# The third unit of a SwiGLU's first phase as a two-sided unit: three of its eight pairs by seven products instead of eight

## The chip, the core and the metric

The kernel runs on one core of a Trainium2 chip, in one launch. The metric is the device time of that launch in microseconds; it took 2192.04 us as the median of three runs (2191.01 to 2192.64).

The engines meant below: TensorE (PE) multiplies a 128x128 stationary operand with up to 512 columns and adds into a bank of PSUM; VectorE (DVE) and ScalarE (ACT) work element by element and read the banks; SyncE (SP) issues the transfers (DMA) from the chip's memory, in order. There are eight banks of 128x512 f32. An engine takes its instructions in the order that was laid down when the program was built, and waits at an instruction until what it needs is there.

## The reference, cut to what matters

Two layers on 256 tokens of width 2048. Each has a mixer and then a SwiGLU of hidden width 5632, in float32. The change is inside the SwiGLU:

```python
def swiglu(x, w_gate, w_up, w_down):
    return (jax.nn.silu(x @ w_gate) * (x @ w_up)) @ w_down

x = layer_norm(DN_ALPHA * x + y, ln_mix_g[layer], ln_mix_b[layer])
f = swiglu(x, ffn_w_gate[layer], ffn_w_up[layer], ffn_w_down[layer])
x = layer_norm(DN_ALPHA * x + f, ln_ffn_g[layer], ln_ffn_b[layer])
```

## The kernel before, in words

Float32 precision is kept by splitting: a weight piece `raw` is copied by ScalarE into a rounded `whi` (L127), VectorE makes the rest `wlo = raw - whi` (L128), and x is held in the same two parts (xTh, xTl). A product is then three matmuls, lo x hi, hi x hi and hi x lo (`mm3`, L292). The 256 tokens are two groups of 128 ("tok").

The hidden width is cut into eleven **units** of 512 columns, and these into three phases (`PHASES`): units 0 to 2, 3 to 6, 7 to 10. A phase computes its units (gate and up projection, silu, product, transposed into yT) and then its share of the down projection, n = 0 to 3, which is added to the residual.

A unit needs 16 k tiles of 128 rows for gate and for up. It goes by eight **pairs** of k tiles. The first phase's units are "whole" (`whole`): eight **halves** (weight pieces of 128x1024, 0.5 MB: two k tiles of one side) for gate, then eight for up, twelve matmuls to a half. The units of the other phases are "two-sided" (`unit`, L454 on): gate and up of a pair are handled together, into four sums c11, c21, c12, c22 (token by side). Three of the pairs (`SEVEN` = 5, 6, 7; two in a phase's last unit) are done by seven products in place of eight, a 2x2 scheme over (two tokens) x (two sides). They need forms of x (sums and differences of x's quarters, `forms_of`, made once a layer and kept) and of the weights (`load_seven`), and four more sums p1, p5, p6, p7:

```python
raw = sp.tile([P, 4, NCH], F32, tag="rs", name="rs", bufs=1)
z = sp.tile([P, 4, NCH], F32, tag="z", name="z", bufs=1)
last_load[0] = nc.sync.dma_start(raw, src).ins
nc.scalar.copy(hi[:, :3], raw[:, :3])
nc.vector.tensor_tensor(z[:, :2], raw[:, 0:3:2], raw[:, 3:4].to_broadcast([P, 2, NCH]), op=add)
nc.vector.tensor_tensor(z[:, 2], z[:, 0], raw[:, 2], op=add)
nc.vector.tensor_tensor(z[:, 3], z[:, 2], raw[:, 1], op=add)
nc.vector.tensor_tensor(lo[:, :3], raw[:, :3], hi[:, :3].bitcast(F32), op=sub)
split(hi[:, 3:], lo[:, 3:], z)
```

So a two-sided load is one transfer of 1 MB into `rs`, of which there is one buffer; three sums of 1024, 512 and 512 columns (L445 to L447); two copies on ScalarE (1536 and 2048 columns) and two splits on VectorE (1536 and 2048). The next load can go out when the last sum has read `rs`. Its parts `sh`, `sl` have two buffers. The forms of x lie in the tiles `xs` and `fs`, which share the buffers of `rs` and `z`, and are split into `fmh`, `fml`.

**Memory.** The weight halves use a ring of buffers: four in `wp`, and until the first phase's units are over seven more (layer 0; in layer 1 three more, and four that were kept) in a pool beside the mixer's room `mix_pool`, which also holds `gam`, `bet` and the tile `sil`. After the third unit `close_mix` gives that memory back, the pool `sp` for the two-sided units opens in it, and the forms of x are made in steps (`make`), spread over the halves of the first down phase. `raw` has four buffers.

**Banks.** PSUM is used in two ways (`open_banks`). In "uses": three `acc`, two `tr` (transposes), three `mx`. In "sides": four `aside` and four `bside`; a unit takes the four of one side for its c sums, and the other four serve first the transposes of the unit before and then p1, p6, p5, p7. The switch to "sides" comes after the third unit.

**Order.** A scheduler lays down each engine's queue when the program is built, by the order of the code and by priority: a load and its split stand some 400 instructions ahead of their place, as far as buffers allow, and `tc.high_priority(offset=1000)` moves other parts forward. `issue_after(low[-1])` puts a piece behind the last split. `later` holds work that is due after so many halves (`half_done`): the transposes of a unit (`transpose4`), and `make`.

Of the kernel before, what the change touches and what calls it, by code (L numbers as in the profile page):

```python
# [11 lines left out]
F32 = mybir.dt.float32  # L12
# [6 lines left out]
P = 128  # L19
# [4 lines left out]
NCH = 512  # L24
# [42 lines left out]
HELD = 6  # L67
FREE = 7
PHASES = ((0, 1, 2), (3, 4, 5, 6), (7, 8, 9, 10))


SEVEN = (5, 6, 7)
PAIRS_FIRST = (0, 1, 2, 3, 5, 4, 6, 7)
PAIRS = (0, 1, 5, 2, 3, 6, 4, 7)
PAIRS_LAST = (0, 1, 5, 2, 6, 3, 4, 7)
# [5 lines left out]
def trunk(ctx: ExitStack, tc: tile.TileContext, a, out):  # L81
# [9 lines left out]
    def open_banks(kind):  # L91

        if banks:
            banks["stack"].close()
        stack = ctx.enter_context(ExitStack())
        pool = stack.enter_context(tc.tile_pool(name="ps", bufs=1, space=PSUM, reuse_waits="tile"))
        banks.update(stack=stack, pool=pool, kind=kind, side=0)
# [22 lines left out]
    def mxp():  # L120
        return bank("mx", 3)
# [26 lines left out]
    first = [True]  # L148
# [33 lines left out]
    later = []  # L182
# [91 lines left out]
    def transpose4(src, hi, lo, ahead_by=0):  # L274
        t = trp()
        for k in range(4):
            transpose(t[:, k * P : (k + 1) * P], src[:, k * P : (k + 1) * P], ident)
        v = t.rearrange("p (k t) -> p k t", k=4)
        with tc.high_priority(offset=ahead_by):
            split(hi, lo, v)  # L280
# [174 lines left out]
    def unit(sp, pairs, sevens, w, lhs, forms, yT, opening):  # L455

        b = {n: side_bank() for n in ("c11", "c21", "c12", "c22")}
        begun = set()
        left = {n: 4 * (len(pairs) - len(sevens)) // 2 for n in b}
        for _, _, n in SEVEN_ORDER:  # L460
            left[n] = left.get(n, 0) + len(sevens)

        def product(name, x, wt):
            left[name] -= 1
            mm3(b[name], x, wt, name not in begun, left[name] == 0)
            begun.add(name)

        behind = [low[-n] if opening and n else None for n in BEHIND]
        for p in pairs:
            if p in sevens:  # L470
                if "p1" not in b:
                    b.update((n, side_bank(True)) for n in ("p1", "p6", "p5", "p7"))
                wt = load_seven(sp, w[p], behind.pop(0))
                for i, x, name in SEVEN_ORDER:
                    product(name, forms[p][x], wt(i))
            else:
                for n, ks in ((0, (2 * p, 2 * p + 1)), (1, (2 * p + 1, 2 * p))):
                    hi, lo = load_half(w[p][:, 2 * n : 2 * n + 2])
                    for tok in range(NT):
                        for kk in range(2):  # L480
                            product(f"c{tok + 1}{n + 1}", lhs(tok, ks[kk]), (hi[:, kk, :], lo[:, kk, :]))
                    half_done()
        with tc.high_priority(offset=1000):
            g0, w_, v, x = (sp.tile([P, NCH], F32, tag=n, name=n, bufs=1) for n in ("g0", "g1", "u0", "u1"))
            nc.scalar.copy(g0, b["p1"])  # L485
            nc.vector.tensor_tensor(w_, g0, b["p6"], op=sub)
            nc.vector.tensor_tensor(v, w_, b["p5"], op=add)
            nc.vector.tensor_tensor(w_, w_, b["p7"], op=add)
            nc.vector.tensor_tensor(x, w_, b["p5"], op=add)
            nc.vector.tensor_tensor(g0, g0, b["c11"], op=add)  # L490
            nc.scalar.activation(g0, g0, AF.Silu)
            nc.vector.tensor_tensor(v, b["c12"], v, op=sub)
            nc.vector.tensor_tensor(w_, w_, b["c21"], op=add)
            nc.scalar.activation(w_, w_, AF.Silu)
            nc.vector.tensor_tensor(x, b["c22"], x, op=sub)

            banks["side"] ^= 1
            for tok, (g, u) in enumerate(((g0, v), (w_, x))):
                nc.vector.tensor_tensor(g, g, u, op=mult)
                s = slice(tok * P, (tok + 1) * P)  # L500
                later.append([2 + tok, lambda g=g, s=s: transpose4(g, yT[0][:, :, s], yT[1][:, :, s], 1000)])

    def ffn(layer, xT, res, mix_pool, close_mix, keep, last):
        lhs = x_lhs(xT)
        w = a[f"gu{layer}"]

        def whole(c, pool, first):

            gouts = [acc() for _ in range(NT)]
            sil = {}  # L510

            def silu(tok):
                sil[tok] = pool.tile([P, NCH], F32, tag="sil", name="sil", bufs=3)
                nc.scalar.activation(sil[tok], gouts[tok], AF.Silu)

            mm_chunk([(w[c, i][:, :2], (2 * i, 2 * i + 1)) for i in range(8)], lhs, gouts, tok_major=first, after=silu)

            uouts = [mxp() for _ in range(NT)]
            y = new_yT()

            def gated(tok):
                with tc.high_priority(offset=1000):
                    nc.vector.tensor_tensor(sil[tok], sil[tok], uouts[tok], op=mult)
                s = slice(tok * P, (tok + 1) * P)
                later.append([(2 if c == PHASES[0][-1] else 4) + tok, lambda: transpose4(sil[tok], y[0][:, :, s], y[1][:, :, s])])

            mm_chunk([(w[c, i][:, 2:], (2 * i + 1, 2 * i)) for i in range(8)], lhs, uouts, after=gated)
            return y

        stack = ExitStack()  # L530
        forms, making = {}, []

        def make():
            with tc.issue_after(low[-1]):
                if next(making[0], "end") is None:
                    later.append([3, make])

        nxt = cdp = None
        groups = {}
        for pi, chunks in enumerate(PHASES):  # L540
            end = pi == len(PHASES) - 1
            for c in chunks:
                if pi == 0:
                    groups[c] = whole(c, mix_pool, c == 0)
                else:
                    groups[c] = new_yT()
                    pairs = PAIRS_FIRST if c == chunks[0] else PAIRS_LAST if c == chunks[-1] else PAIRS
                    sevens = SEVEN[:-1] if c == chunks[-1] else SEVEN
                    unit(sp, pairs, sevens, w[c], lhs, forms, groups[c], c == chunks[0])
            if pi == 0:  # L550
                close_mix()
                sp = later_pool(stack, f"sp{layer}")
                open_banks("sides")
                making.append(forms_of(sp, xT, forms))
                later.append([2, make])
            gl = [groups[c] for c in chunks]
            if end:
                stack.close()
                open_banks("uses")
                cdp = None if last else keep("cdc")  # L560
                open_ring(keep(f"er{layer}"), 4)
                open_ring(later_pool(stack, f"e{layer}"), 3)
                fp = later_pool(stack, f"g{layer}")
                nxt = None if last else new_xT()
            stats = new_stats()
            evac, norm = residual_tools(res, None, None, None, stats)
            for n in range(4):
                if cdp and n == 1:
                    consts.extend(cd_constants(cdp))
                if end and n == 1:  # L570
                    evac, norm = residual_tools(res, *load_gb(fp, layer, "ffn"), stats)
                outs = [acc() for _ in range(NT)]
                halves = [(a[f"down{layer}"][n, 2 * c + i], two(4 * ci + 2 * i)) for ci, c in enumerate(chunks) for i in range(2)]

                def after(tok):
                    with tc.high_priority(offset=1000 if end and n == 3 else 0):
                        evac(tok, n, outs[tok], pi == 0, end)
                        if end and n == 3:
                            norm(tok, nxt, out if last else None)

                mm_chunk(halves, y_lhs(gl), outs, tok_major=(end and n == 3), after=after)
            if not end:
                banks["side"] ^= 1
        if end:
            rings.pop()
            stack.close()
        return nxt
# [416 lines left out]
    xT = new_xT()  # L1004
# [11 lines left out]
    def later_pool(stack, name):  # L1016
        return stack.enter_context(tc.tile_pool(name=name, bufs=1, reuse_waits="tile"))
# [22 lines left out]
    xT = layer_end(0, a["ab_out"], AB_OUT_GROUPS, yT, False)  # L1040
# [119 lines left out]
```

## Time and profile before

| | |
|---|---|
| median of three runs | 2192.04 us |
| the profiled execution's own time | 2190.72 us |
| its span on the core | 2188.9 us |
| granted TensorE clock, mean | 0.998 |
| PE busy | 2170.7 us (99%) |
| DVE busy | 1558.8 us (71%) |
| ACT busy | 1051.3 us (48%) |

The profile comes from one execution; its span starts with the program's first instruction on the core and ends with the last, and the time around it is 1.8 us more. Matmul records overlap, since a matmul's record holds its latency: what a matmul costs is read from one start to the next. In a row, `acc<-whi,xTl` says that a matmul reads whi and xTl and adds into acc; numbers of buffers are left out in the profile.

### The profile page before, as it was taken

The page shows a single profiled execution, that of the slowest core. Times are in us where ns is not written, and L with a number is a line of the kernel's source. Part 1 is how long each engine was busy: PE and PEld are TensorE (multiplying, and loading weights), DVE is VectorE, ACT ScalarE, POOL GpSimd, SP SyncE. Part 2 cuts the span into 40 slices and gives each one's busy share as a digit, 9 for nine tenths or more (in the row PEclk, how much of TensorE's full clock was granted, in tenths as well). Part 3 has the DMA queues.
Part 4 walks back from the last instruction along what each step waited for, and adds up shares of the span by engine and source line. Part 5 has one row for each costly group of instructions (what it writes and reads, how often), then busy time and mean ns, then how long its engine had stood idle before and what let it go on. Part 6 is the DMA issues. An engine that isn't in the chain of part 4 may idle for free.

```text
span 2188.9 us, 26626 instructions
## 1 busy us (share of the span) xinstructions
PE 2170.7 (99%) x10048; PEld 1804.7 (82%) x10048; DVE 1558.8 (71%) x1954; ACT 1051.3 (48%) x1278; POOL 51.7 (2%) x51
## 2 busy tenths in 40 slices
PE   9999999999999999999999999999999999999997
PEld 7888888888888888888888888888888888888886
DVE  6886688577537787577876776667367896768765
ACT  6445544545435455444545554455344554445442
POOL 0000000000000000000000300000000000000000
PEclk9999999999999999999999999999999999999999
DMA  8555546584736565565549553747456555655563
GB/s 294 161 164 180 167 132 190 195 287 138 237 125 219 188 208 189 189 230 185 199 157 305 165 190 106 235 150 253 143 187 232 185 187 188 222 173 200 172 238 122
DMA packets 112850, 420.64 MB, mean 192 GB/s; under 512 B 13776, under 2 KB 16848, under 8 KB 105808
## 3 DMA queue, kind: packets, MB, share of 16 engines
q1 hardware_dynamic: 112720, 418.93, 57.8%
q8 instruction: 79, 1.29, 0.2%
q14 instruction: 51, 0.42, 0.1%
HBM read 416.78 MB, written 2.10 MB: 191 GB/s over the span
## 4 chain that ended last, share of the span: by engine, by line
PE 96%; DMA 1%; DVE 1%; ACT 0%; issue 0%; SPq 0%; DVEq 0%; ACTq 0%
PE acc L292 41%; PE bside L292 23%; PE aside L292 21%; PE mx L292 7%; PE mx L729 1%; PE tr L124 1%; DMA raw<-in_down 1%; DVE wlo L128 0%; DMA rs<-in_gu 0%; PE mx L775 0%; DMA raw<-in_ab_in 0%; PE bside L124 0%; PE aside L124 0%; PE mx L985 0%; ACT whi L127 0%
## 5 line engine op out<-in xcount | busy, mean ns | idle before, releaser
L128 DVE TENSOR_TENSOR wlo<-raw,whi 128x1024 fp32r<-128x1024 f32 (+1 forms) x673 | 817.8, 1224 | 438.2 <-ACT whi L127 431.2
L127 ACT CAST whi<-raw 128x1024 fp32r<-128x1024 f32 (+1 forms) x673 | 703.7, 1052 | 820.5 <-PE acc L292 262.3
L292 PE MATMUL acc<-whi,xTl 128*128 128x512 f32 x864 | 342.8, 397 | 4.8 <-ACT whi L127 4.8
L292 PE MATMUL acc<-whi,xTh 128*128 128x512 f32 x864 | 340.0, 393 | 0.0
L292 PE MATMUL acc<-wlo,xTh 128*128 128x512 f32 x864 | 337.9, 393 | 0.1
L292 PE MATMUL acc<-whi,yTl 128*128 128x512 f32 x512 | 200.8, 392 | 0.2
L292 PE MATMUL acc<-whi,yTh 128*128 128x512 f32 x512 | 199.6, 390 | 0.0
L292 PE MATMUL acc<-wlo,yTh 128*128 128x512 f32 x512 | 197.7, 390 | 0.0
L292 PEld LDWEIGHTS acc<-whi,xTl 128*128 128x128 f32 x864 | 162.9, 189 | 37.2 <-ACT whi L127 5.7
L292 PEld LDWEIGHTS acc<-wlo,xTh 128*128 128x128 f32 x864 | 162.9, 189 | 33.9 <-DVE wlo L128 1.1
L292 PEld LDWEIGHTS acc<-whi,xTh 128*128 128x128 f32 x864 | 163.1, 189 | 31.1
L292 PE MATMUL bside<-whi,xTl 128*128 128x512 f32 x336 | 131.4, 391 | 0.7 <-ACT g L485 0.6
L292 PE MATMUL bside<-whi,xTh 128*128 128x512 f32 x336 | 131.0, 390 | 0.0
L292 PE MATMUL aside<-whi,xTl 128*128 128x512 f32 x336 | 131.0, 390 | 0.0
L292 PE MATMUL aside<-whi,xTh 128*128 128x512 f32 x336 | 130.9, 390 | 0.0
L292 PE MATMUL bside<-wlo,xTh 128*128 128x512 f32 x336 | 128.1, 390 | 0.0
L292 PE MATMUL aside<-wlo,xTh 128*128 128x512 f32 x336 | 128.1, 390 | 0.0
L292 PEld LDWEIGHTS acc<-wlo,yTh 128*128 128x128 f32 x512 | 96.1, 188 | 20.6 <-DVE wlo L128 0.5
L292 PEld LDWEIGHTS acc<-whi,yTl 128*128 128x128 f32 x512 | 96.2, 188 | 20.0 <-DVE res L310 0.5
L292 PEld LDWEIGHTS acc<-whi,yTh 128*128 128x128 f32 x512 | 96.2, 188 | 19.4
L128 DVE TENSOR_TENSOR sl<-z,sh 128x2048 fp32r<-128x2048 f32 x44 | 100.7, 2289 | 6.4 <-ACT sh L127 5.7
L292 PE MATMUL bside<-whi,yTl 128*128 128x512 f32 x256 | 99.8, 390 | 0.0
(266 smaller groups left out, 3414.3 us busy)
## 6 DMA issues: line engine op xcount, KB each, us to landing
raw<-in_gu SPq DMA_DIRECT2D x264, 512.0 KB, 4.7
raw<-in_down SPq DMA_DIRECT2D x176, 512.0 KB, 3.9
raw<-in_ab_in SPq DMA_DIRECT2D x127, 512.0 KB, 4.2
rs<-in_gu SPq DMA_DIRECT2D x44, 1024.0 KB, 5.9
raw<-in_cd_in SPq DMA_DIRECT2D x40, 512.0 KB, 4.2
raw<-in_ab_out SPq DMA_DIRECT2D x32, 512.0 KB, 4.4
raw<-in_cd_out SPq DMA_DIRECT2D x32, 512.0 KB, 4.2
bias<-in_na_bias SPq DMA_DIRECT2D x32, 64.0 KB, 4.2
```

The source lines that it names most:

```text
L124: return nc.tensor.transpose(o, src, eye)
L127: nc.scalar.copy(hi, src)
L128: return nc.vector.tensor_tensor(lo, src, hi.bitcast(F32), op=sub).ins
L292: ins = nc.tensor.matmul(o, lhs[a], rhs[b], start=start and n == 0, stop=stop and n == 2)
L729: nc.tensor.matmul(m[:, 2 * h + s, :], kk[:, h, s * P : (s + 1) * P], qq[:, h, r * P : (r + 1) * P], start=True, stop=True,)
```

## The change

In each layer the third unit (c = 2) is no longer whole but two-sided, with `PAIRS` and `SEVEN` as in the middle of the other phases: pairs 0, 1, 5, 2, 3, 6, 4, 7, of which 5, 6 and 7 go by seven products. For this, the mixer's room is closed and `sp` is opened when the sixth half of the second unit (c = 1) is done (`change_rooms`), `make` runs after each further half, and the switch to the side banks comes after the second unit. The gate's tiles of the second unit are taken from `sp` (`g0`, `g1`). The transposes of the second unit are due two halves into the third unit instead of four. The rest is as before.

```diff
         def whole(c, first):
...
             def silu(tok):
-                sil[tok] = pool.tile([P, NCH], F32, tag="sil", name="sil", bufs=3)
+
+                if sps:
+                    sil[tok] = sps[0].tile([P, NCH], F32, tag=f"g{tok}", name=f"g{tok}", bufs=1)
+                else:
+                    sil[tok] = mix_pool.tile([P, NCH], F32, tag="sil", name="sil", bufs=3)
...
-                later.append([(2 if c == PHASES[0][-1] else 4) + tok, lambda: transpose4(sil[tok], y[0][:, :, s], y[1][:, :, s])])
+                later.append([(4 if first else 2) + tok, lambda: transpose4(sil[tok], y[0][:, :, s], y[1][:, :, s])])
...
         def make():
             with tc.issue_after(low[-1]):
                 if next(making[0], "end") is None:
-                    later.append([3, make])
+                    later.append([1, make])
+
+        def change_rooms():
+            close_mix()
+            sps.append(later_pool(stack, f"sp{layer}"))
+            making.append(forms_of(sps[0], xT, forms))
+            later.append([1, make])
...
-                if pi == 0:
-                    groups[c] = whole(c, mix_pool, c == 0)
+                if c < 2:
+                    groups[c] = whole(c, c == 0)
+                    if c == 0:
+                        later.append([6, change_rooms])
+                    else:
+                        open_banks("sides")
                 else:
                     groups[c] = new_yT()
...
+                    pairs, sevens = PAIRS, SEVEN
+                    if pi and c == chunks[0]:
+                        pairs = PAIRS_FIRST
+                    elif pi and c == chunks[-1]:
+                        pairs, sevens = PAIRS_LAST, SEVEN[:-1]
+                    unit(sps[0], pairs, sevens, w[c], lhs, forms, groups[c], pi and c == chunks[0])
-            if pi == 0:
-                close_mix()
-                sp = later_pool(stack, f"sp{layer}")
-                open_banks("sides")
-                making.append(forms_of(sp, xT, forms))
-                later.append([2, make])
```

VectorE in layer 0, around the end of the second unit and the start of the third. The numbers are those of buffers. Before, from the second unit's gate product (sil and the bank mx) to its first transposed part yTl:

```order
L523 TENSOR_TENSOR sil_5022<-sil_5022,mx_5026 128x512
L523 TENSOR_TENSOR sil_5024<-sil_5024,mx_5027 128x512
L128 TENSOR_TENSOR wlo_5382<-raw_5380,whi_5381 128x1024
L128 TENSOR_TENSOR wlo_5400<-raw_5398,whi_5399 128x1024
L128 TENSOR_TENSOR wlo_5418<-raw_5416,whi_5417 128x1024
L128 TENSOR_TENSOR wlo_5436<-raw_5434,whi_5435 128x1024
L128 TENSOR_TENSOR wlo_5454<-raw_5452,whi_5453 128x1024
L128 TENSOR_TENSOR yTl_5029<-tr_5250,yTh_5028 128x4x128
```

And of the changed kernel, the last twelve rows to the same part, which now comes from a side bank (g1 is the gate product, 5398 and 5467 are the buffers of the unit's second and third two-sided load):

```order
L528 TENSOR_TENSOR g1_5032<-g1_5032,mx_5035 128x512
L448 TENSOR_TENSOR z_5401<-z_5401,rs_5398 128x512
L129 TENSOR_TENSOR wlo_5273<-raw_5271,whi_5272 128x1024
L129 TENSOR_TENSOR sl_5400<-z_5401,sh_5399 128x2048
L446 TENSOR_TENSOR z_5470<-rs_5467 128x1024
L129 TENSOR_TENSOR wlo_5328<-raw_5326,whi_5327 128x1024
L447 TENSOR_TENSOR z_5470<-z_5470,rs_5467 128x512
L448 TENSOR_TENSOR z_5470<-z_5470,rs_5467 128x512
L129 TENSOR_TENSOR wlo_5346<-raw_5344,whi_5345 128x1024
L129 TENSOR_TENSOR yTl_5037<-bside_5239,yTh_5036 128x4x128
L129 TENSOR_TENSOR wlo_5364<-raw_5362,whi_5363 128x1024
L129 TENSOR_TENSOR yTl_5037<-bside_5264,yTh_5036 128x4x128
```

Between the gate product and yTl there were only low parts of weight halves; now the sums of two two-sided loads and a split stand there too. In layer 1 the same rows stand in another order: a low part ahead of the third load's first sum, and yTl two rows behind that sum, ahead of its other two sums.

TensorE in layer 0 at the fifth half of the third unit. Before, it is the gate part of a whole unit, with the second unit's transposes (tr) ahead of the half 5259:

```order
L124 MATMUL tr_5250<-ident_72,sil_5022 128x128 x4
L292 MATMUL acc_5176<-whi_5258,xTl0_3822 128x512
L292 MATMUL acc_5176<-whi_5258,xTh0_3820 128x512
L292 MATMUL acc_5176<-wlo_5259,xTh0_3820 128x512
...
L292 MATMUL acc_5177<-whi_5258,xTl1_3823 128x512
```

The changed kernel begins its first pair by seven products there (pair 5, weights sh_5294 and sl_5295), from the first sum, p1 (bside_5289), over p6 (bside_5290) to p5 (bside_5291):

```order
L293 MATMUL bside_5289<-sh_5294,xTl0_3822 128x512
L293 MATMUL bside_5289<-sh_5294,xTh0_3820 128x512
L293 MATMUL bside_5289<-sl_5295,xTh0_3820 128x512
L293 MATMUL bside_5290<-sh_5294,fml_5116 128x512
L293 MATMUL bside_5290<-sh_5294,fmh_5115 128x512
L293 MATMUL bside_5290<-sl_5295,fmh_5115 128x512
L293 MATMUL aside_5199<-sh_5294,xTl0_3822 128x512
L293 MATMUL bside_5291<-sh_5294,fml_5116 128x512
L293 MATMUL bside_5291<-sh_5294,fmh_5115 128x512
L293 MATMUL bside_5291<-sl_5295,fmh_5115 128x512
```

The second unit's transposes have written the first two of the four `bside` banks (bside_5239, bside_5264); p1 and p6 take the other two, p5 the first of these, and p7 (bside_5292), which comes eleven matmuls later, the second. The first matmul into p5 therefore waits for yTl<-bside_5239 of the order above, and the first into p7 for yTl<-bside_5264. In layer 1 p7 comes fourteen matmuls later.

## Rows read from the trace of the kernel before

**Rows 1.** The page: busy time of the engines (us, share of the span, count) and the two groups that prepare a weight half (line, engine, operation, names, shapes, count | busy us, mean ns of one | idle before it).

```profile
PE 2170.7 (99%) x10048; PEld 1804.7 (82%) x10048; DVE 1558.8 (71%) x1954; ACT 1051.3 (48%) x1278; POOL 51.7 (2%) x51
...
L128 DVE TENSOR_TENSOR wlo<-raw,whi 128x1024 fp32r<-128x1024 f32 (+1 forms) x673 | 817.8, 1224 | 438.2 <-ACT whi L127 431.2
L127 ACT CAST whi<-raw 128x1024 fp32r<-128x1024 f32 (+1 forms) x673 | 703.7, 1052 | 820.5 <-PE acc L292 262.3
```

**Rows 2.** The two longest waits of TensorE in the whole trace: who waited for whom, us in total, times, longest.

```profile
PE acc L292 <- ACT whi L127: 4.8, 1, 4.8
PE mx L292 <- DVE ptl L128: 1.2, 1, 1.2
```

**Rows 3.** Stretches of the span: the third unit of layer 0 as it is now (611 to 655 us) and a two-sided unit of the second phase (790 to 840 us); busy us of each engine with its count, then the granted clock, the DMA share and GB/s.

```profile
611.00:655.00 44.00, 44.00 (x202) 36.37 (x202) 14.54 (x15) 11.10 (x14) 0.00 (x0) 1.00 0.34 106
...
790.00:840.00 50.00, 50.00 (x226) 41.22 (x225) 44.40 (x44) 27.10 (x26) 0.00 (x0) 1.00 0.53 182
```

**Rows 4.** TensorE in order of time, from the third unit of layer 0: start us, us, engine, line, operation, names, count.

```profile
609.70 0.39 PE L292 MATMUL acc<-wlo,xTh 128*128 128x512 f32 x1
...
612.42 0.39 PE L292 MATMUL acc<-wlo,xTh 128*128 128x512 f32 x1
612.65 0.60 PE L124 MATMUL tr<-ident,sil 128*128 128x128 f32 x4
...
613.32 0.39 PE L292 MATMUL acc<-whi,xTh 128*128 128x512 f32 x1
```

**Rows 5.** VectorE in order of time in a two-sided unit, same columns.

```profile
794.25 0.69 DVE L446 TENSOR_TENSOR z<-z,rs 128x512 f32<-128x512 f32 x1
794.86 1.75 DVE L448 TENSOR_TENSOR sl<-rs,sh 128x1536 fp32r<-128x1536 f32 x1
796.52 0.69 DVE L447 TENSOR_TENSOR z<-z,rs 128x512 f32<-128x512 f32 x1
797.12 1.22 DVE L128 TENSOR_TENSOR wlo<-raw,whi 128x1024 fp32r<-128x1024 f32 x1
798.26 0.68 DVE L486 TENSOR_TENSOR g<-g,bside 128x512 f32<-128x512 f32 x1
799.05 0.69 DVE L487 TENSOR_TENSOR u<-g,bside 128x512 f32<-128x512 f32 x1
...
800.25 2.28 DVE L128 TENSOR_TENSOR sl<-z,sh 128x2048 fp32r<-128x2048 f32 x1
802.45 0.68 DVE L488 TENSOR_TENSOR g<-g,bside 128x512 f32<-128x512 f32 x1
...
814.06 0.69 DVE L128 TENSOR_TENSOR yTl<-aside,yTh 128x512 fp32r<-128x512 f32 x1
```

**Rows 6.** The last operation of the forms of x: operation, count, duration ns min/median/max, first and last start.

```profile
L425 DVE TENSOR_TENSOR fs<-xs,fs x2: 551/552/552, 677.1 to 1625.1; 128x384 f32<-128x384 f32 x2
```

**Rows 7.** ScalarE in order of time: the copies of a two-sided pair.

```profile
1049.46 1.48 ACT L444 CAST sh<-rs 128x1536 fp32r<-128x1536 f32 x1 [1.83 <-DMA rs<-in_gu]
...
1054.80 1.92 ACT L127 CAST sh<-z 128x2048 fp32r<-128x2048 f32 x1 [2.43 <-DVE z L447]
```

**Rows 8.** SyncE’s queue in order of time: the issues around four 1 MB loads (rs).

```profile
674.01 3.05 SPq L168 DMA_DIRECT2D raw<-in_down  x2
677.72 0.33 SPq L443 DMA_DIRECT2D rs<-in_gu  x1
679.45 0.33 SPq L168 DMA_DIRECT2D raw<-in_down  x1
...
794.37 0.33 SPq L168 DMA_DIRECT2D raw<-in_gu  x1
797.29 0.33 SPq L443 DMA_DIRECT2D rs<-in_gu  x1
798.38 0.33 SPq L168 DMA_DIRECT2D raw<-in_gu  x1
...
1622.02 3.05 SPq L168 DMA_DIRECT2D raw<-in_down  x2
1625.67 0.81 SPq L443 DMA_DIRECT2D rs<-in_gu  x1
1627.46 3.09 SPq L168 DMA_DIRECT2D raw<-in_down  x2
...
1757.02 2.06 SPq L168 DMA_DIRECT2D raw<-in_gu  x2
1760.56 0.33 SPq L443 DMA_DIRECT2D rs<-in_gu  x1
1761.69 0.33 SPq L168 DMA_DIRECT2D raw<-in_gu  x1
```

**Rows 9.** The 1 MB loads from issue to landing, us min/median/max: all 44, and then the four of [rows 8] by themselves, in the same order (issued at 677.7, 797.3, 1625.7, 1760.6).

```profile
DMA to landing us min/median/max: 4.6/5.9/8.7
...
DMA to landing us min/median/max: 7.2/7.2/7.2
...
DMA to landing us min/median/max: 4.8/4.8/4.8
...
DMA to landing us min/median/max: 6.1/6.1/6.1
...
DMA to landing us min/median/max: 6.0/6.0/6.0
```

More of the change, by code (lines that the diff above doesn't have):

```diff
@@ L505, in ffn, with whole @@
         w = a[f"gu{layer}"]
-        def whole(c, pool, first):
+        def whole(c, first):
             gouts = [acc() for _ in range(NT)]
@@ L530, in ffn @@
         stack = ExitStack()
-        forms, making = {}, []
+        forms, making, sps = {}, [], []
         def make():
@@ L542, in ffn @@
             for c in chunks:
-                if pi == 0:
-                    groups[c] = whole(c, mix_pool, c == 0)
+                if c < 2:
[4 more added lines that the diff above has]
+                        open_banks("sides")
                 else:
                     groups[c] = new_yT()
-                    pairs = PAIRS_FIRST if c == chunks[0] else PAIRS_LAST if c == chunks[-1] else PAIRS
-                    sevens = SEVEN[:-1] if c == chunks[-1] else SEVEN
-                    unit(sp, pairs, sevens, w[c], lhs, forms, groups[c], c == chunks[0])
-            if pi == 0:
-                close_mix()
-                sp = later_pool(stack, f"sp{layer}")
-                open_banks("sides")
-                making.append(forms_of(sp, xT, forms))
-                later.append([2, make])
+                    pairs, sevens = PAIRS, SEVEN
[4 more added lines that the diff above has]
+                    unit(sps[0], pairs, sevens, w[c], lhs, forms, groups[c], pi and c == chunks[0])
             gl = [groups[c] for c in chunks]
```

## The prediction

> **What bounds the kernel now.** I read the page first. TensorE is busy for 2170.7 of 2188.9 us, and VectorE for 71% [rows 1]. Then I asked for TensorE's waits: outside the start, where it waits for the first weights, the longest one is 1.2 us, in another mixer [rows 2]. So the time is the number of matmuls times their step, and a change here can win only by leaving matmuls out, and lose only by making TensorE wait. The step is in the timeline: twelve matmuls start between 609.70 and 612.42, which is 2.72 us for a half (one 128x1024 weight piece) and 0.2268 us for a matmul; a group of four transposes adds 0.44 us (612.42 to 613.32, less two steps) [rows 4]. The record of 0.39 us is its latency, not its cost. Last I read the stretches. In the present third unit VectorE works 14.5 of 44 us, in a two-sided unit 44.4 of 50 [rows 3]: the change turns a stretch where VectorE has much room into one where it has little, and the price, if there is one, is to be looked for there.
>
> **The gain.** A pair by eight products takes 2 tokens x 2 k tiles x 2 sides x 3 = 24 matmuls, a pair by seven takes 7 x 3 = 21. The third unit has 192 matmuls now; five pairs by 24 and three by 21 make 183. The transposes stay. Over two layers 18 matmuls go: 18 x 0.2268 = 4.1 us. More than that cannot be gained in these units, since TensorE does not wait there now.
>
> **The work that is only moved.** The forms of x (two sums, four differences, one split) leave the first down phase and enter the second unit. The ring of weight buffers falls from eleven (layer 0) to four there, one unit earlier. Four halves are 4 x 2.72 = 10.9 us of cover, as much as the later phases have, which run without a wait. I price both at nothing; what hides them is TensorE's second unit itself, with one half of 1.22 us on VectorE and 1.05 us on ScalarE [rows 1] in every 2.72 us. The six more 1 MB loads replace twelve of 0.5 MB, so the bytes are the same.
>
> **What is added: a chain to the third unit's first seven-product pair.** The second order fence shows that the sum p5 writes a bank that the transposes of the second unit have used, and so has to wait until VectorE has read it (yTl). The first fence shows where that reading stands: behind the first operation of the third two-sided load. That load cannot be issued before the second one's last sum, nor the second before the first's, since there is one buffer. I set 0 at the third unit's first matmul and follow this chain on VectorE, with these steps from start to start: 1.14 us for 1024 columns, 0.60 for 512, 1.66 for 1536, 2.20 for 2048, and 0.79 for 512 directly ahead of an operation that reads its result [rows 5].
>
> TensorE asks for the bank after 4 halves, two groups of transposes and 7 matmuls: 10.89 + 0.88 + 1.59 = 13.4 us. The eighth half of the second unit's gate part, which is its last, begins 9 halves before 0, at -24.5. The seventh half's buffer is free then: ScalarE's copy (1.05) and VectorE's low part (1.14) end near -22.2, and two form operations of 0.55 us [rows 6] at -21.1, when the first load goes out.
>
> How long a load takes depends on its neighbours. All 44 took 4.6 to 8.7 us, the middle one 5.9 [rows 9]. Those with a 0.5 MB load issued about 1 us ahead of them and another 1.7 us behind (677.7 and 1625.7) took 7.2 and 6.1; with one 2.9 us ahead and one 1.1 us behind (797.3) 4.8; with two some 3.5 and 1.8 us ahead and one 1.1 us behind (1760.6) 6.0 [rows 8, 9]. By the order of the changed kernel the three loads meet just these three neighbourhoods, in this order. I take 7.2 (layer 0) and 6.1 (layer 1) for the first, 4.8 and 6.0 for the others.
>
> Layer 0: the first load lands at -13.9, and with 0.1 us for the signal VectorE begins at -13.8. Sum, low part, sum, split of 1536, sum: 1.14 + 1.14 + 0.60 + 1.66 + 0.69 = 5.2, to -8.6, and the second load is out; it lands at -3.8. VectorE gets there at -3.0, after two low parts, the split of 2048 and a low part (0.60 + 2.28 + 2.20 + 1.14 from the last sum's start at -9.3), so this landing is hidden by 0.7 us. Then sum, split of 1536, low part, sum, low part, the two gate products of the second unit, sum: 1.14 + 1.66 + 1.14 + 0.60 + 1.14 + 1.20 + 0.69 = 7.6, to 4.5. The third load lands at 10.5. VectorE has a low part and a split ahead of it; the split waits for ScalarE's copy of 1.92 us [rows 7], and is done at 8.7, so the landing counts. From 10.6: 1.14 + 1.14 + 0.79 + 0.60 + 1.14 + 0.69 = 5.5, to 16.1. TensorE waits 16.1 - 13.4 = 2.8 us. The second bank (p7) is asked for 2.5 us after it goes on, and is free by then.
>
> Layer 1: the first load is 1.1 us shorter, which moves all to the front by as much, and the scheduler put the bank's reading three places further forward. VectorE has read it at 9.55 + 1.14 + 1.14 + 0.69 = 12.5, 0.9 us ahead of time; the second one at 15.5, against 16.5. No wait.
>
> Sum: -4.1 + 2.8 + 0 = -1.3 us. The profiled execution takes 2190.7 us, so 2189.4; against the median of the three runs, 2192.0, it is 2190.7, which I predict. The bounds of the wait come from the loads alone. With 4.6 us for the first and third it is nothing. With 8.7 for all three it is 2.8 + 1.5 + 3.2 + 2.7 = 10.2 us in layer 0 and 2.6 + 3.2 + 2.7 - 0.9 = 7.6 in layer 1, which would be 2205.8; no neighbourhood that took over 8 us is met here, and I stay with the nearest rows.
>
> A rule speaks for a longer chain. In [rows 5] an operation of 1.22 us is followed by the next 1.14 us after its start, so records overlap by 0.08 us. The Trainium skill, "VectorE: DVE Perf Modes", section "The DRAIN you can't avoid", says that the next operation does not start until the pipe is empty (and that one which is not held starts earlier). By whole durations the 22 steps of the chain that are not hidden would take 22 x 0.08 = 1.8 us more: waits of 4.6 and 0.9 us, and 2193.4 us in all. The rows show the shorter step at each place that I looked at, so I keep it.
>
> At the end of the third unit the last pair is now one by seven products, and its side sums must leave the banks before the down phase writes them. The first of these banks is read by one ScalarE copy that can start 18 matmuls (4.1 us) before it is needed; I price this at nothing, and at the 0.7 us of one 512-column operation if that cover fails.
>
> **Rivals.**
> No wait at all. The first and third load together would take 2.8 us less than my 13.2 (the second is hidden), as two of 5.2 us do. For it: the smallest is 4.6, and the schedule was laid out for some such time. Against it: a lone load is what took 4.7 to 4.8, and these are not alone. Time: 2192.0 - 4.1 = 2187.9.
> Slower: the second load lands late too. One buffer serves all three loads, so each landing hands its delay on. It decides from the point where the second takes over 5.5 us. If all three take 7.2 us, layer 0 waits 2.8 + 1.7 + 1.2 = 5.7 and layer 1 waits 1.1 + 1.7 + 1.2 - 0.9 = 3.1; -4.1 + 8.8 = +4.7, so 2196.7. For it: VectorE is at 89% in a two-sided unit [rows 3]. Against it: the same neighbourhood gave 4.8 [rows 9].
> Whole durations on VectorE, as worked out above: 2193.4.
>
> **How the numbers follow.** The forecast gets 0.62, no wait 0.24, the late second load 0.07, whole durations 0.05, and 0.02 stays for waits that I don't see. The first two and the fourth hold 0.91, and lie from 2187.9 to 2193.4; with the spread of the runs (about 0.8 us each way) the range is 2187.4 to 2193.6, which leaves under 2 in 10 outside. 0.2% is 4.4 us, about what a measurement of this kernel can tell from no change. The full gain of 4.1 us lies just inside, so faster by more needs that case and a little luck: 0.07. Slower by more needs the late second load: 0.06. The rest, 0.87, is no change.
>
> **What would show it.** Eighteen matmuls fewer and the same step confirm the gain. In the list of TensorE's waits there should be one of 2 to 4 us for VectorE's yTl in layer 0's third unit, at its first seven-product pair, and none or a small one in layer 1. The three loads ahead should take about 7, 5 and 6 us, and VectorE should sit idle for some 2 us ahead of the third one's first sum. I am wrong if there is no such wait, if TensorE waits for a weight half in the second unit (then the smaller ring was not enough), or if the waits pass 8 us together.

## The result, and the profile after

The changed kernel takes 2196.08 us (median of 13 runs, 2193.79 to 2200.09), and the kernel before, in the same comparison, 2191.71 (13 runs, 2189.64 to 2193.70). The ratio is 1.0019, 95% interval 1.0012 to 1.0027: slower by 4.4 us, where 1.3 us less was forecast. The wait that the forecast spoke of is there, at the place that it named, but it is longer; a second one stands in layer 1, where none was expected; and the first one brings the clock down.

Of the profile after (own time 2196.08 us, clock 0.997), the page's first part, and then the waits of TensorE that the profile lists:

```profile
span 2194.2 us, 26598 instructions
PE 2169.3 (99%) x10030; PEld 1802.1 (82%) x10030; DVE 1589.1 (72%) x1988; ACT 1059.0 (48%) x1280; POOL 55.4 (3%) x51
```

```profile
PE bside L293 <- DVE yTl L129: 5.9, 2, 4.2
PE acc L293 <- ACT whi L128: 5.2, 2, 4.8
PE mx L293 <- DVE ptl L129: 1.2, 1, 1.2
PE aside L293 <- ACT g L486: 0.9, 1, 0.9
```

Eighteen matmuls fewer, as worked out, yet the span is 5.3 us longer. Against [rows 2], the first line is new: two waits, 5.9 us together, for VectorE's part of a transposed bank. The last line comes up below. In TensorE's order of time, the place in layer 0's third unit:

```profile
614.76 0.39 PE L293 MATMUL aside<-sh,xTl 128*128 128x512 f32 x1
619.32 0.50 PE L293 MATMUL bside<-sh,fml 128*128 128x512 f32 x1 [4.18 <-DVE yTl L129]
...
619.89 0.63 PE L293 MATMUL bside<-sl,fmh 128*128 128x512 f32 x1
620.31 0.63 PE L293 MATMUL aside<-sh,xTh 128*128 128x512 f32 x1
620.74 0.63 PE L293 MATMUL aside<-sl,xTh 128*128 128x512 f32 x1
...
623.30 0.40 PE L293 MATMUL aside<-sl,xTh 128*128 128x512 f32 x1
623.53 0.40 PE L293 MATMUL bside<-sh,fml 128*128 128x512 f32 x1
```

From 614.76 to 619.32 are 4.56 us; less a step of 0.2268 us, 4.34 us are lost. The bracket's 4.18 is the same wait counted from the end of the record before. Then the step is 0.43 us instead of 0.23 for eight matmuls (from 619.89 to 623.30), and they lose 0.20 us each, 1.6 us together. The stretches show why (busy us of each engine with its count, granted clock, DMA share, GB/s):

```profile
615.00:620.00 5.00, 0.82 (x4) 0.59 (x4) 4.96 (x7) 1.04 (x1) 0.00 (x0) 0.99 0.35 116
620.00:623.50 3.50, 3.50 (x10) 2.75 (x9) 2.13 (x3) 0.00 (x0) 0.00 (x0) 0.53 0.87 262
623.50:628.00 4.50, 4.50 (x21) 3.69 (x20) 2.24 (x2) 3.80 (x3) 0.00 (x0) 1.00 0.38 137
```

The granted clock is 0.53 in the middle stretch, nearly all of it at the lower of the two levels (1.2 of 2.4 GHz), after TensorE had stood still and had just begun again; and 0.99 and 1.00 before and after. The recorded clocks of all executions fit: the mean over the whole launch is 0.997 in 9 of the 13 executions of the changed kernel, and in one of the 63 of the kernel before in the comparisons below (0.998 or 0.999 in the others).

Why did TensorE wait? VectorE in the same place:

```profile
605.35 0.68 DVE L448 TENSOR_TENSOR z<-z,rs 128x512 f32<-128x512 f32 x1
605.96 1.22 DVE L129 TENSOR_TENSOR wlo<-raw,whi 128x1024 fp32r<-128x1024 f32 x1
608.01 2.29 DVE L129 TENSOR_TENSOR sl<-z,sh 128x2048 fp32r<-128x2048 f32 x1 [0.84 <-ACT sh L128]
613.85 1.22 DVE L446 TENSOR_TENSOR z<-rs 128x1024 f32<-128x1024 f32 x1 [3.54 <-DMA rs<-in_gu]
...
618.58 0.68 DVE L129 TENSOR_TENSOR yTl<-bside,yTh 128x512 fp32r<-128x512 f32 x1
```

It stands idle for 3.54 us at the first sum of the third load, while the bank that TensorE wants is waiting for a reader five operations further back in the same queue. The chain of the work that ended last runs through the load: it was issued at 606.06, when the last sum of the second load had read `rs`.

```profile
605.43 0.61 DVE z L448
...
606.06 7.69 DMA rs<-in_gu
...
618.67 0.61 DVE yTl L129
...
619.32 1.19 PE bside L293 x3
```

In layer 1 the same happens on a smaller scale: VectorE idles 2.22 us for the third load, TensorE loses 1.86 us (a bracket of 1.70), and the matmuls behind it keep the step of 0.23 us.

```profile
1571.22 0.50 PE L293 MATMUL bside<-sh,fml 128*128 128x512 f32 x1 [1.70 <-DVE yTl L129]
```

The account: -4.1 (matmuls) + 4.34 + 1.86 (waits) + 1.6 (half clock) + 0.2 (one late step behind each wait) = +3.9. The small waits at the start of later units, for what reads the banks of the unit before and for a low part sl, sum to 2.8 us in this trace and to 1.2 in that of before, which makes +5.5; the spans differ by 5.3. Of the 2.8, 1.0 is for ScalarE's copy g, and most of the rest for VectorE's g.

### The profile page after: what moved, and what is told of

Same layout as the page of the kernel before. It is cut to its first block, busy times and chain, and to the rows that moved or that the text cites. A ratio compares the mean times of both kernels' runs of the same rounds, so it can differ in the third digit from the quotient of the medians.

```text
span 2194.2 us, 26598 instructions
## 1 busy us (share of the span) xinstructions
PE 2169.3 (99%) x10030; PEld 1802.1 (82%) x10030; DVE 1589.1 (72%) x1988; ACT 1059.0 (48%) x1280; POOL 55.4 (3%) x51
## 4 chain that ended last, share of the span: by engine, by line
PE 93%; DVE 3%; DMA 2%; issue 1%; ACT 0%; SPq 0%; DVEq 0%; ACTq 0%
PE acc L293 41%; PE aside L293 24%; PE bside L293 20%; PE mx L293 4%; DMA rs<-in_gu 2%; PE mx L741 1%; PE tr L125 1%; DVE wlo L129 1%; DVE sl L129 0%; PE mx L787 0%; PE aside L125 0%; PE bside L125 0%; PE mx L997 0%; DVE sl L449 0%; DMA raw<-in_ab_in 0%
## 5 line engine op out<-in xcount | busy, mean ns | idle before, releaser
L129 DVE TENSOR_TENSOR wlo<-raw,whi 128x1024 fp32r<-128x1024 f32 (+1 forms) x661 | 800.8, 1222 | 377.5 <-ACT whi L128 372.6
L293 PE MATMUL acc<-whi,xTl 128*128 128x512 f32 x800 | 317.4, 397 | 5.2 <-ACT whi L128 5.2
L293 PE MATMUL acc<-whi,xTh 128*128 128x512 f32 x800 | 314.8, 393 | 0.0
L293 PE MATMUL acc<-wlo,xTh 128*128 128x512 f32 x800 | 312.6, 393 | 0.1
L293 PE MATMUL aside<-whi,xTl 128*128 128x512 f32 x416 | 162.8, 391 | 1.1 <-ACT g L486 0.9
L293 PE MATMUL aside<-whi,xTh 128*128 128x512 f32 x416 | 162.2, 390 | 0.0
L293 PE MATMUL aside<-wlo,xTh 128*128 128x512 f32 x416 | 159.0, 390 | 0.0
L445 ACT CAST sh<-rs 128x1536 fp32r<-128x1536 f32 x50 | 74.2, 1483 | 100.6 <-DMA rs<-in_gu 42.8
L129 DVE TENSOR_TENSOR sl<-z,sh 128x2048 fp32r<-128x2048 f32 x50 | 114.4, 2289 | 10.0 <-ACT sh L128 9.2
L128 ACT CAST sh<-z 128x2048 fp32r<-128x2048 f32 x50 | 95.7, 1913 | 34.3 <-DVE z L448 34.0
```

The source lines that it names most:

```text
L128: nc.scalar.copy(hi, src)
L129: return nc.vector.tensor_tensor(lo, src, hi.bitcast(F32), op=sub).ins
L293: ins = nc.tensor.matmul(o, lhs[a], rhs[b], start=start and n == 0, stop=stop and n == 2)
```

## Experiments

Theory A is the account above. Theory B: the work moved into the second unit costs the time. Theory C: VectorE has too much to do in the third unit, and a wait taken away comes back elsewhere. Each time stands beside that of the kernel before in the same comparison: 2192.05 us for the first four experiments, 2191.53 for the next two, 2191.95 for the last.

**1. The reader ahead of the sums.**

```diff
-    def load_seven(sp, src, behind):
+    def load_seven(sp, src, behind, after_read=False):
...
+            if after_read:
+                order.enter_context(tc.issue_after(reads[-1]))
             nc.vector.tensor_tensor(z[:, :2], raw[:, 0:3:2], raw[:, 3:4].to_broadcast([P, 2, NCH]), op=add)
...
-                wt = load_seven(sp, w[p], behind.pop(0))
+                wt = load_seven(sp, w[p], behind.pop(0), first_phase and p == sevens[-1])
```

`reads` holds VectorE's low parts of the whole units' transposes; its last entry is the reading of the second bank. One thing came out other than the text below says: TensorE's order changed a little. The three matmuls into p5 stand one place earlier than in the changed kernel, and in layer 1 those into p7 three places; so the banks are asked for slightly earlier, which does not help this kernel. ScalarE's and SyncE's queues are the same.

> One edit to the changed kernel: in the first phase VectorE's three sums of the third two-sided load (and its splits) are put behind the reading of the second transpose bank; loads, matmuls and their order stay. Theory A (the bank's reader stands behind a late 1 MB load; that wait, 4.3 us in layer 0 and 1.9 in layer 1, and the half clock after the first one, 1.6 us, are the loss): no wait for yTl over 0.3 us, no half clock in the third unit, the whole gain of 4.1 us, 2187.6 us where the kernel before takes 2191.7. Theory B (the forms and the room, moved into the second unit, cost the time): 2196, as the changed kernel. Theory C (VectorE has too much to do in the two-sided third unit; a wait taken away at one place comes back at the last seven-product pair): 2192 to 2195, with a new wait for sl or sh of the third load.

Measured 2188.97 us, ratio 0.9984 (0.9975 to 0.9993): 3.1 us less than before, where A gives 4.1 less, B 4 more, and C up to 3 more. The interval (1.5 to 5.5 us less) holds A's value and neither of the others. VectorE in layer 0:

```profile
610.72 2.35 DVE L129 TENSOR_TENSOR wlo<-raw,whi 128x1024 fp32r<-128x1024 f32 x2
612.99 0.68 DVE L129 TENSOR_TENSOR yTl<-bside,yTh 128x512 fp32r<-128x512 f32 x1
613.59 1.21 DVE L129 TENSOR_TENSOR wlo<-raw,whi 128x1024 fp32r<-128x1024 f32 x1
614.72 0.68 DVE L129 TENSOR_TENSOR yTl<-bside,yTh 128x512 fp32r<-128x512 f32 x1
615.32 1.21 DVE L450 TENSOR_TENSOR z<-rs 128x1024 f32<-128x1024 f32 x1
```

The third load still took 7.3 us, but the banks are read at 612.99 and 614.72, and the sum finds its data there. TensorE waits for no yTl, and its clock stays up in the third unit. So a third load of over 7 us costs nothing when nothing that is wanted stands behind it; its own pair is the unit's last. This kernel is faster than the one before and, by the ratios (0.9984 against 1.0019), than the changed one.

**2. The first seven-product pair later.**

```diff
+                    elif pi == 0:
+                        pairs = (0, 1, 2, 5, 3, 6, 4, 7)
```

> The changed kernel with the third unit's pairs in the order 0, 1, 2, 5, 3, 6, 4, 7: TensorE comes to the first seven-product pair two halves (5.4 us) later, while VectorE's order round the loads stays nearly as it is. Theory A: 5.4 us are more than either wait, so both go, with the half clock: 2187.6 us. Theory B: 2196. Theory C: 2192 to 2195, since VectorE has as much to do as before.

Measured 2192.03 us, ratio 1.0001 (0.9992 to 1.0009): the gain is lost, and A's 2187.6 was wrong. The waits, and the place:

```profile
PE acc L293 <- ACT whi L128: 5.0, 2, 4.8
PE aside L293 <- DVE wlo L129: 2.3, 1, 2.3
```

```profile
613.60 0.39 PE L293 MATMUL aside<-whi,xTh 128*128 128x512 f32 x1
616.26 0.50 PE L293 MATMUL aside<-wlo,xTh 128*128 128x512 f32 x1 [2.28 <-DVE wlo L129]
...
617.68 0.63 PE L293 MATMUL aside<-whi,xTl 128*128 128x512 f32 x1
```

```profile
617.00:620.50 3.50, 3.50 (x11) 2.73 (x10) 3.50 (x5) 0.44 (x1) 0.00 (x0) 0.54 0.60 198
```

VectorE there, at the third load's first sum:

```profile
613.85 1.23 DVE L446 TENSOR_TENSOR z<-rs 128x1024 f32<-128x1024 f32 x1 [3.56 <-DMA rs<-in_gu]
614.99 1.22 DVE L129 TENSOR_TENSOR wlo<-raw,whi 128x1024 fp32r<-128x1024 f32 x1
```

I had looked at the bank alone. The late load (7.7 us) holds up the whole queue of VectorE, and the low part of the next weight half, which is wanted here first, stands behind the same sum. The wait is 2.4 us, eight matmuls at half clock follow, 1.6 us: 4.0, against the gain of 4.1. In layer 1, where the third load took 7.2 us, there is no wait. The time is also what C named; but in the first experiment VectorE had the same work to do, and there the wait did not come back. Theory A must read: whatever stands behind that sum in VectorE's queue is late, the bank or a weight part, whichever TensorE comes to first.

**3. Only what is moved.**

```diff
-                if c < 2:
+                if c < 3:
...
-                    else:
+                    elif c == 2:
                         open_banks("sides")
```

> Only what is moved: the room closes and the forms of x are made in the second unit, but the third unit stays whole (192 matmuls), and the switch to the side banks comes after it. Theory A: as the kernel before, 2191.7 us, no wait of TensorE over 0.5 us in the second and third unit. Theory B: the moved work costs what the gain hides, so 8 us more than the kernel before, about 2200. Theory C: 2191.7.

Measured 2192.92 us, ratio 1.0003 (0.9994 to 1.0012). No wait in the second and third unit. B is out: its 8 us would be a ratio of 1.0037.

**4. Two pairs by seven.**

```diff
+                    elif pi == 0:
+                        sevens = SEVEN[1:]
```

> The changed kernel with two pairs by seven products (6 and 7) in the third unit in place of three: 12 matmuls fewer than the kernel before, two 1 MB loads ahead of the banks' reading in place of three, none of them between the second one and the reader. Theory A: no wait, 12 x 0.2268 = 2.7 us less than the kernel before, 2189.0 us. Theory B: 2197.5. Theory C: between 2190 and 2193.

Measured 2188.60 us, ratio 0.9987 (0.9979 to 0.9996), 3.5 us less (2.9 by the ratio), with A's 2.7 inside the interval. No wait in the third unit, nor a fallen clock. The 1 MB load that now goes out third belongs to the fourth unit; it took 7.9 us, and its first sum stands behind both readings of the banks.

**5. The remedy in layer 0 alone.** The edit is shown against the first experiment's kernel.

```diff
-                    unit(sps[0], pairs, sevens, w[c], lhs, forms, groups[c], pi and c == chunks[0], pi == 0)
+                    unit(sps[0], pairs, sevens, w[c], lhs, forms, groups[c], pi and c == chunks[0], pi == 0 and layer == 0)
```

> As the first experiment (third load's sums behind the reading of the banks), but in layer 0 only; layer 1 stays as in the changed kernel. Theory A: no wait and no half clock in layer 0's third unit, the wait of about 1.9 us at layer 1's stays and does not bring the clock down: -4.1 + 1.9, so 2.2 us less than the kernel before, 2189.9 where that takes 2192.1. If the half clock came of the wait in layer 1 too, 2191.5. Theory B or C (the time is lost elsewhere): 2194 to 2196.

Measured 2189.86 us, 1.7 us less than before; ratio 0.9994 (0.9985 to 1.0004). Expected were 2.2 less. The one wait for yTl that is left is layer 1's:

```profile
1561.08 0.39 PE L295 MATMUL aside<-sh,xTl 128*128 128x512 f32 x1
1563.19 0.50 PE L295 MATMUL bside<-sh,fml 128*128 128x512 f32 x1 [1.72 <-DVE yTl L129]
1563.52 0.39 PE L295 MATMUL bside<-sh,fmh 128*128 128x512 f32 x1
1563.75 0.40 PE L295 MATMUL bside<-sl,fmh 128*128 128x512 f32 x1
```

The matmuls behind this wait of 1.9 us keep the full step. The changed kernel lay 4.4 us above before, this one 1.7 below: layer 0's wait cost some 6.0 us (5.5 by the ratios), where wait and half clock of the trace add up to 5.9. The intervals (some 2 us either way) are too wide for the half clock's 1.6 us to be read from the times; the traces show it.

**6. The third load without neighbours.** Three 0.5 MB loads are left out and their buffers filled with zeros.

```diff
+                if empty:
+                    nc.gpsimd.memset(raw[:, s, :], 0.0)
+                else:
...
-                    hi, lo = load_half(w[p][:, 2 * n : 2 * n + 2])
+                    hi, lo = load_half(w[p][:, 2 * n : 2 * n + 2], empty=first_phase and (p, n) in ((2, 1), (3, 0), (3, 1)))
```

> The changed kernel without the three 0.5 MB loads that are issued round the third two-sided load (3.5 and 1.8 us ahead of it, 1.1 us behind): GpSimd fills those buffers with zeros, so three weight halves of the third unit (pair 2's second, both of pair 3) are left out of the result in each layer. Order on VectorE and TensorE as in the changed kernel. Theory A with neighbours as the cause of the late landing: the third load takes 4.7 to 5.3 us in place of 7.5 to 7.7, as lone ones do; the wait in layer 0 falls from 4.3 to 1.3 to 2.0 us, that in layer 1 is gone, no half clock, 2189.3 to 2190 where the kernel before takes 2192.1. Theory A with a load that is slow by itself (its place in memory, its size): 7 us or more as before, waits of 3.5 and over 1 us, 2195 to 2196.

The third load's time from issue to landing, layer 0 and layer 1, each in a view of its own, and the wait that is left:

```profile
DMA to landing us min/median/max: 4.7/4.7/4.7
...
DMA to landing us min/median/max: 4.7/4.7/4.7
```

```profile
PE bside L296 <- DVE yTl L129: 1.2, 1, 1.2
```

The load falls by 3 us, the wait in layer 0 from 4.34 to 1.33, that in layer 1 goes, and so does the half clock. The neighbours are what makes the load late; which of the three does it, this run does not tell. The time is 2190.98 us, ratio 0.9996 (0.9987 to 1.0005): 0.6 us less than before, where 2.1 to 2.8 were expected; the interval reaches to 2.8 less. The small waits at the start of later units come to 2.9 us in its trace, 1.7 more than in that of before, which would close most of the difference; whether they do so in the median can't be read from one trace.

**7. Those small waits.** In experiment 3 TensorE, VectorE, ScalarE and SyncE have the same order as before in each layer from the second phase's second unit on, and yet its trace has 3.0 us of such waits, that of before 1.2. So their sum differs between executions with the same order, and how much of it the change brings is open. The last line of the list of waits after shows one of them: ScalarE idles for a 1 MB load, and the copy of a bank stands behind it.

```profile
1098.97 1.49 ACT L445 CAST sh<-rs 128x1536 fp32r<-128x1536 f32 x1 [4.47 <-DMA rs<-in_gu]
1100.36 1.04 ACT L128 CAST whi<-raw 128x1024 fp32r<-128x1024 f32 x1
1101.30 0.57 ACT L486 COPY g<-aside 128x512 f32<-128x512 f32 x1
```

So the same remedy was tried there, on top of experiment 1, on ScalarE's queue alone:

```diff
+                if opens and taken[0]:
+                    later_cast.enter_context(tc.issue_after(taken[0]))
                 nc.scalar.copy(hi[:, :3], raw[:, :3])
...
-            nc.scalar.copy(g0, b["p1"])
+            taken[0] = nc.scalar.copy(g0, b["p1"]).ins
```

> The first experiment's kernel, and besides in every two-sided unit ScalarE's copy of the bank p1 is put ahead of its copy (sh) of the next unit's first 1 MB load. This is to show whether the small waits of TensorE at the start of the later units (1.2 us in all in the profile before, 1.6 to 3.4 in the changed kernels, for ScalarE's g) are the same thing as the wait in the third unit: a bank's reader that stands behind a late load. If so, they go (under 0.5 us in all), and the time is 1 to 2.5 us below the first experiment's 0.9984 of the kernel before, about 2187 where that takes 2192. If they come of something else, or if the later copy of the load delays the next unit's first seven-product pair, the waits stay or move and the time is 2189 or more.

Measured 2207.09 us, ratio 1.0073 (1.0060 to 1.0087): 15 us slower, more than I had allowed for. The new waits:

```profile
PE aside L296 <- DVE g L495: 3.3, 2, 1.6
PE bside L296 <- DVE g L495: 3.0, 2, 1.6
PE bside L296 <- DVE sl L129: 2.3, 2, 1.1
```

ScalarE's copy is gone from the list, and VectorE's readers of the banks have come in its place, and with them the low part of the load itself (sl), which the text above named as the other outcome. Most of the small waits had been for VectorE's g from the start (2.0 of 2.9 us in experiment 1), so an edge on ScalarE's queue need not take them away: in experiment 1 one such g stood behind a split of the load that ended at 844.3, long after ScalarE's copy of the bank had ended at 837.6. The readers stand behind the sum of the next unit's first load, as they did in experiment 1; but the edge made the scheduler lay out four queues anew, and that load now goes out 2.0 us later (at 829.7 in place of 827.7):

```profile
836.99 1.23 DVE L454 TENSOR_TENSOR z<-rs 128x1024 f32<-128x1024 f32 x1 [5.11 <-DMA rs<-in_gu]
...
841.73 0.68 DVE L495 TENSOR_TENSOR g<-g,bside 128x512 f32<-128x512 f32 x1
```

In experiment 1 the sum began at 834.75 and the reader at 840.02. So the same mechanism, a bank's reader behind a late load, is at work here, and the edge on one queue did not cure it. How much of the 15 us comes of the later load and how much of the new order of the queues was not taken apart. The profiled execution took 2202.55 us, so its trace shows only some two thirds of the loss. In one place the clock fell again:

```profile
2059.40:2062.90 3.50, 3.50 (x9) 2.73 (x10) 3.50 (x4) 0.80 (x3) 0.00 (x0) 0.52 0.68 192
```

A wait of 1.8 us ends there (2059.38), and 1 us ahead of it lies one of 0.7 us. After the waits of 1.8, 1.8 and 1.5 us in three other units, which had one of 0.3 us or none shortly ahead of them, the clock stays at 1.00.

## Why the prediction was wrong, step by step

**Right.** The gain: 18 matmuls, and the step is unchanged. The moved work: nothing that experiment 3 can tell from no cost (1.3 us less to 2.6 more), and no wait where it now stands. The end of the third unit: nothing, since no wait stands there in the trace. The place of the wait, and the chain to it: with 0 at the third unit's first matmul (601.55), the third load goes out at 4.5, as worked out, and TensorE asks at 13.4. From the first sum to the end of the bank's reading VectorE takes 5.4 us (613.85 to 619.26); 5.5 were worked out by start-to-start steps. The whole durations of the six operations (1.22, 1.22, 0.68, 0.69, 1.22, 0.68) sum to 5.7. The Trainium skill, "VectorE: DVE Perf Modes", section "The DRAIN you can't avoid", says that the next operation does not start until the pipe is empty, which would ask for at least these, and that one which is not held starts earlier; the trace fits the exception and not the rule.

**Wrong: the term for the third load.** "I take 7.2 (layer 0) and 6.1 (layer 1) for the first, 4.8 and 6.0 for the others." The first took 7.2 in both layers, the second 4.8 and 5.3, the third 7.7 and 7.5:

```profile
DMA to landing us min/median/max: 7.2/7.2/7.2
...
DMA to landing us min/median/max: 4.8/4.8/4.8
...
DMA to landing us min/median/max: 7.7/7.7/7.7
```

In layer 0 the error of the wait is the third load: 1.7 us more than I took, and the wait is 4.34 in place of 2.8. In layer 1 it is that load (1.5 more) and the first one (1.1 more), against a slack of 0.9: 1.7 by this sum, 1.86 measured. The 6.0 was one row [rows 8, 9], for a neighbourhood (two loads 3.5 and 1.8 us ahead, one 1.1 us behind) that the trace of before met four times: 6.1, 6.1 and 6.0 us, and the fourth 7.6. I had read all four before I predicted, and the prediction shows and uses a 6.0 alone; the row that would have warned me was left out without a reason.

```profile
DMA to landing us min/median/max: 7.6/7.6/7.6
```

In the trace after, the six loads with that neighbourhood took 6.35 to 7.7 us. In these rows a neighbourhood gives a span of times and not one time; the least of it stood in the sum, in a chain of three loads in which only the second has slack ahead of it in layer 0 (0.7 us). With 7.6 in place of 6.0 the sum would have been +1.0 us, by 1.6 more in layer 0 and 0.7 in layer 1.

**Wrong: what the wait does to the clock.** No term of the sum, no rival and no bound had it. I treated a wait as the time that TensorE stands still. In layer 0 it cost another 1.6 us afterwards. The forecast wait of 2.8 us would probably have carried it too, since in experiment 2 one of 2.4 us did; with that alone the forecast would have been about +0.3 us.

Together: 1.5 us more wait in layer 0, 1.9 in layer 1, 1.6 of half clock and 0.2 of late steps are 5.2 of the 5.7 us between forecast and measurement. The rest lies within the 1.6 us by which the small waits grew in the trace, for which the sum had no term.

**The rivals.** The late second load named nearly the right time (2196.7), and got 0.07, but by luck, for its reason did not come about: the second load took about what I gave it. I had asked which load would be late, and should have asked how likely it is that any of three is. The range ended at 2193.6 although the bounds that I had worked out reached 2205.8; I let one row of 6.0 us cut it.

## What to carry to other kernels

Where an engine's queue holds the first reader of a load, look up everything that stands behind it and is wanted soon: a late load delays all of it, and a reader whose own result is wanted late belongs behind the rest. Price such a load by the spread of all rows in the same surroundings, not by one, and add to a long wait of TensorE what the lower clock costs afterwards (1.6 us in the third unit here). After pinning one queue, read the others again, since a scheduler may lay them out anew.

## What the runs showed of the hardware

A 1 MB load that shares its time with three of 0.5 MB took 7.5 to 7.7 us in the changed kernel (6.9 to 7.9 in the other traces with the same neighbours at that place), and 4.7 at the same place in the program without them.

TensorE's granted clock fell to its lower level after waits of 4.3 and 2.4 us in the third unit, each time shortly after the work had begun again, and stayed there for eight matmuls; after those of 1.3 and 1.9 us there it did not. Length alone does not decide it: in experiment 7 it fell after a wait of 1.8 us that had one of 0.7 us shortly ahead of it, and not after two others of 1.8 us. The slow step is 0.427 us (620.31 to 623.30, seven steps). The Trainium skill, "TensorE: Matmul & The Clock Gate", section "Wait — 56ns, not 53.3ns?", gives 426.7 ns for 512 columns at the low clock; the trace agrees.
